# A two-layer decoder trunk on one core: the head reordered around modulation chunks, mixers and fillers

## The chip, the cores and the metric

The kernel runs on one core of a Trainium2 chip. The metric is the device time of one execution in microseconds. Three runs of the kernel before gave 560.85, 561.9 and 562.68 us; their median is 561.9 us.

## The reference

The input `x` is 256 tokens of 1024 channels, and `c` is one vector of 1024. Layer 0 mixes tokens by causal pooling, layer 1 by attention over one block of 256 tokens, and each is followed by a dense MLP with a squared ReLU.

```
c_act = silu(c)
for i in (0, 1):
    sh1, sc1, g1, sh2, sc2, g2 = split(c_act @ w_mod[i] + b_mod[i])     # six chunks of 1024
    h = rmsnorm(x, norm_mix[i]) * (1 + sc1) + sh1
    y = pool_mixer(h) if i == 0 else attention(h)
    x = x + g1 * y
    h = rmsnorm(x, norm_mlp[i]) * (1 + sc2) + sh2
    x = x + g2 * (relu(h @ w_up[i])**2 @ w_down[i])
out = rmsnorm(x, norm_final)

pool_mixer: channels in 4 groups of 256, windows 2, 4, 8, 16:
    (trailing mean of h over the window - h) @ w_pool[group], times pool_scale
```

## The kernel before

Activations stand transposed: 8 tiles of 128 channels by 256 tokens. All large weights come in transfers of 1 MB (16 tiles of 128x128) through SP's queue into five buffers (`RAW_BUFS`), in the order of `load_order` (L108). `issue` (L181) sends the next transfer; it is called when one has been used up, so transfer k+5 goes out once transfer k has been multiplied. A small transfer (a pool weight, or half of the first MLP weight) is sent along with the one ahead of it.

From the first MLP on, weights run as a stream: ScalarE casts each half transfer to a high part (`split_hi`, L250), VectorE subtracts to get a low part (`split_lo`, L256), and TensorE takes three matmuls for each tile (`mm_sum`, L274): high weights by high activations, high by low, low by high. `next_tile` (L620) hands out the tiles in a fixed order and runs whatever was put down for that tile by `later` (L612). This stream starts with the `m0u` matmuls (the first up-projection) and lasts to the end of the kernel.

The head is everything ahead of that stream, and the change lies in it. Its order on each engine is the order of the program; there is no planner. It does this:

- `cb` (L233 to L238): TensorE spreads silu(c) over all partitions, ScalarE copies it to `cact` (L553), for later chunks of the modulation that VectorE computes.
- The first norm: ScalarE squares `x` (L451), VectorE folds the squares by four adds (L452 to L455), TensorE sums them over partitions (`Rms.sums`, L376), ScalarE and VectorE take the reciprocal root (`rstd`, L386), TensorE spreads it (`spread`, L400), ScalarE copies it to `R` (`to_sbuf`, L408).
- The modulation of layer 0, as pairs of chunks. `PAIRS` (L50) names them: `sh0` to `sh3` are scale and shift of one channel group, `g32` and `g10` the gates of two groups each, `mlp0` to `mlp2` scale and shift for the MLP. A pair is two transfers, each holding half of the contraction for both chunks. `take` (L526) runs the products of one transfer (`pair_mm`, L302: 16 matmuls, 32 records) and calls `issue`. `given` (L529) lets VectorE pick the column out of the PSUM tile (`pair_out`, L313: four products, each with a read of its accumulator).
- For each channel group, 3 to 0: `normed` (L539) multiplies `x` by the root, `mixer` (L472) applies gain and shift on ScalarE and adds 4, 3, 2 or 1 shifted copies on VectorE, `pool_products` (L501) multiplies by the pool weights on TensorE. The loop at L543 finishes a group's mixer before it starts the next.
- `pool_out` (L514) adds the gated result to `x` and squares it, `pool_sums` (L522) sums the squares for the second norm `n1`; then `mlp0_in` (L593) makes the first MLP inputs, high and low part.
- `keep_warm` (L332) runs matmuls whose result nobody reads ("fillers"), at places chosen by hand.

Of the kernel before, what the change touches and what calls it, by code (L numbers as in the profile page):

```python
# [15 lines left out]
P = 128  # L16
# [91 lines left out]
def load_order():  # L108
    order = []

    def pair(name):
        order.extend(("c", name, i) for i in range(2))

    for j in GROUPS:
        pair(f"sh{j}")
        order.append(("p", j))
    pair("g32")
    pair("g10")
    order.append(("w0a",))
    pair("mlp0")  # L120
    order.extend([("w0b",), ("w", 1)])
    pair("mlp1")
    order.extend([("w", 2), ("w", 3)])
    pair("mlp2")
    order.extend([("w", 4), ("m", 0, 4, 3), ("m", 0, 3, 3), ("w", 5)])
    late = 0
    for h in range(HEAD_STEPS - AHEAD, N_STEPS):
        while late < len(LATE_STEPS) and LATE_STEPS[late] <= h:
            order.append(("m",) + LATE_MODS[late])
            late += 1  # L130
        if (h + AHEAD) % 2 == 0 and h + AHEAD < N_STEPS:
            order.append(("w", (h + AHEAD) // 2))
    return order
# [6 lines left out]
def tile_hybrid_pool_moba(  # L140
# [89 lines left out]
    nc.scalar.activation(ccol, vec[:, V_C : V_C + KD], AF.Silu)  # L230
    nc.scalar.activation(warm, ones, AF.Sqrt)
    cact = const.tile([P, D], F32, name="cact")
    cb = [bank(f"cb{i}") for i in range(2)]  # L233
    for k in range(KD):
        i, a = divmod(k, KD // 2)
        nc.tensor.matmul(
            cb[i][:, a * P : (a + 1) * P], ccol[:, k : k + 1].to_broadcast([P, P]), ident, start=True, stop=True
        )  # L238
# [60 lines left out]

    def pair_mm(name, half, region):  # L302
        w = loaded["c", name, half].rearrange("p (k q n) -> p k q n", k=KD // 2, q=4)
        for k in range(KD // 2):
            c0 = half * KD // 2 + k
            for q in range(4):
                nc.tensor.matmul(
                    region[32 * q : 32 * q + 32, :], ccol[:, c0 : c0 + 1].to_broadcast([P, 32]), w[:, k, q],
                    start=c0 == 0, stop=c0 == KD - 1, skip_group_check=True,
                )  # L310
        issue()

    def pair_out(name, region):  # L313
        for i, key in enumerate(PAIRS[name]):
            layer, m, j = key
            for a in range(2):
                t = tmp.tile([P, 32], F32, tag="pk", bufs=4, name="pk")
                nc.vector.scalar_tensor_tensor(
                    t, region[:, (2 * i + a) * 32 : (2 * i + a + 1) * 32], mod_bias(*key)[:, a : a + 1], pick,
                    op0=ALU.add, op1=ALU.mult, accum_out=mods[layer, m][:, 2 * j + a : 2 * j + a + 1],  # L320
                )
            known.add(key)
# [133 lines left out]
    pma = bank("pma")  # L456
    region = {f"sh{j}": pma[:, j * P : (j + 1) * P] for j in range(4)}
# [56 lines left out]
    def pool_out(g):  # L514
        cols = slice(2 * g, 2 * g + 2)
        nc.vector.tensor_mul(g1[:, cols], mods[0, 2][:, cols], vec[:, V_PSC + 2 * g : V_PSC + 2 * g + 2])
        for n in range(2):
            residual_sum(pools[g][:, n * S : (n + 1) * S], 2 * g + n, g1)
        sq1[g] = al_tile([P, 2, S], f"n1_sq{g}")
        nc.scalar.activation(sq1[g], x[:, 2 * g : 2 * g + 2], AF.Square)  # L520

    def pool_sums(g):  # L522
        for a in range(2):
            n1.sums(sq1[g][:, a], (g, a) == (0, 1))
# [4 lines left out]
    def given(name):  # L529
        pair_out(name, region[name])  # L530
# [3 lines left out]
    rms.spread()
    R = rms.to_sbuf()
    Rb = R.rearrange("p (a b) -> p a b", a=1).to_broadcast([P, 2, S])
    xr = [None] * 4

    def normed(g):  # L539
        xr[g] = al_tile([P, 2, S], f"n0_xr{g}")  # L540
        nc.vector.tensor_mul(xr[g], x[:, 2 * g : 2 * g + 2], Rb)

    for g, nxt in ((3, 2), (2, 1), (1, 0)):  # L543
        normed(g)
        given(f"sh{g}")
        if g == 3:
            keep_warm(2)
        take(f"sh{nxt}", 0)
        weave(mixer(g))
        if g == 3:  # L550
            keep_warm(2)
            for i in range(2):
                nc.scalar.copy(cact[:, i * D // 2 : (i + 1) * D // 2], cb[i])  # L553
        take(f"sh{nxt}", 1)
        pool_products(g)
    normed(0)
    given("sh0")
    weave(mixer(0))
    pool_products(0)
# [30 lines left out]
    gs01 = const.tile([P, KD], F32, name="gs0_4")  # L590


    def mlp0_in(j, R):  # L593
        gain(0, 4, V_NMLP, gs01, 2 * j, 2 * j + 2)
        sh = modv(0, 3, 2 * j)
        u = {}
        for k in (2 * j, 2 * j + 1):
            hl[k] = hl_tile(f"h01_{k}")
            u[k] = tmp.tile([P, S], F32, tag="h", bufs=2, name=f"h01_u{k}")
            nc.vector.scalar_tensor_tensor(u[k], xs[k], gs01[:, k : k + 1], R, op0=ALU.mult, op1=ALU.mult)  # L600
            nc.scalar.activation(hl[k][:, :S], u[k], AF.Identity, bias=sh[:, k : k + 1])
        for k in u:
            nc.vector.scalar_tensor_tensor(
                hl[k][:, S : 2 * S], u[k], sh[:, k : k + 1], hl[k][:, :S].bitcast(F32),
                op0=ALU.add, op1=ALU.subtract,
            )

    now = [0]
    due = {}
# [26 lines left out]
    def up(layer, hl, R):  # L636
        name = f"m{layer}u"
        g = (G_UP0, G_UP1)[layer]
        al = [None] * KF
        banks = {}  # L640

        def done(n):
            nm = f"{name}{n}"
# [46 lines left out]
        for n, k in UP_ORDER[layer]:  # L690
            w = next_tile()
            paired = R is None and n < g and n % 2 == 1
            if k == 0:
                banks[n] = banks[n - 1] if paired else bank(f"{name}{n}")
            t = hl[k]
            if R is None:
                a = S if paired else 0

                last = n % 2 == 1 or n >= g
                mm_sum(  # L700
                    banks[n][:, a : a + S], w, t[:, :S], t[:, S : 2 * S], k == 0 and a == 0, k == KD - 1 and last
                )
# [75 lines left out]
        return run  # L778

    def inputs(j):  # L780
        return lambda: mlp0_in(j, R1)

    mlp0_in(0, R1)
    R1 = n1.to_sbuf()
    split(1)
    head(2, splits(2))
    head(6, splits(3))
    head(12, take_late("mlp1", 0))
    head(19, take_late("mlp1", 1), lambda: given("mlp1"), inputs(1), splits(4))
# [312 lines left out]
```

## Time and profile before

| | |
|---|---|
| median of 3 runs | 561.9 us (560.85 to 562.68) |
| the profiled execution | 559.75 us, its span 558.0 us |
| granted clock, mean of the span | 0.983 |
| TensorE busy | 534.0 us, 96% |
| VectorE busy | 408.9 us, 73% |
| ScalarE busy | 323.1 us, 58% |
| read from HBM | 138.64 MB, 250 GB/s over the span |
| first `m0u` matmul | 60.94 us after the span's start |

The span runs from the first to the last instruction; the time of the execution includes what lies around it. Busy time of TensorE counts every matmul as long as its row says, at whichever clock it ran. The granted clock is 1.00 at full speed (2.4 GHz) and 0.50 at half (1.2 GHz); a value between is a mean over a stretch that holds both. An fp32 matmul has two records.

### The profile page before, as it was taken

To read this page: it belongs to the slowest core of one execution; us is meant where nothing else is said; L and a number is where in the kernel's file an instruction comes from. 1 tells how busy PE (TensorE), PEld (TensorE's weight loads), DVE (VectorE), ACT (ScalarE), POOL (GpSimd) and SP (SyncE) were. 2 spreads that over 40 slices of the span, in tenths; PEclk is the share of its full clock that TensorE was granted. 3 is DMA by queue.
4 is the path that set the end of the run, shared out by engine and by line. 5 is a ranking of instruction groups with operands and counts; after the bars stand their busy time and mean duration, and the time that the engine had idled before them with its cause. 6 is when DMAs were issued, how large, how long until landed. Compare 5 with 4: busy or idle time off the path is not lost.

```text
span 558.0 us, 10792 instructions
## 1 busy us (share of the span) xinstructions
PE 534.0 (96%) x4328; PEld 496.2 (89%) x4328; DVE 408.9 (73%) x830; ACT 323.1 (58%) x602; POOL 2.5 (0%) x18
## 2 busy tenths in 40 slices
PE   5777999999999999999999999999999999999995
PEld 4556899999998888899899999999999998888895
DVE  2644469689987998965899995686887786665641
ACT  3212234678754454454887878566897775444531
POOL 1000000000000000000000000000000000000000
PEclk9896899999999999999999999999999999999999
DMA  8998789748889989984377675434565477677002
GB/s 331 418 369 332 282 320 365 263 158 307 325 308 408 404 309 325 346 332 162 144 260 284 238 284 218 152 137 167 188 230 188 162 275 241 205 278 269 4 0 76
DMA packets 22338, 140.41 MB, mean 252 GB/s; under 512 B 2416, under 2 KB 4608, under 8 KB 5904
## 3 DMA queue, kind: packets, MB, share of 16 engines
q1 hardware_dynamic: 22048, 138.61, 67.5%
q10 hardware_dynamic: 144, 1.05, 0.5%
q8 instruction: 34, 0.56, 0.4%
q14 instruction: 16, 0.13, 0.1%
q0 software_dynamic: 96, 0.06, 0.0%
HBM read 138.64 MB, written 1.07 MB: 250 GB/s over the span
## 4 chain that ended last, share of the span: by engine, by line
PE 92%; DVE 4%; ACT 1%; DMA 1%; issue 1%; DVEq 0%
PE m1d L270 9%; PE m0d L270 9%; PE m1u L276 6%; PE m1u L277 6%; PE m1u L278 6%; PE m0u L276 6%; PE m0u L278 5%; PE m0u L277 5%; PE m0d L271 5%; PE m1d L271 5%; PE qkv L276 5%; PE qkv L277 4%; PE qkv L278 4%; PE wo L276 1%; PE n_rms L381 1%; PE wo L278 1%
## 5 line engine op out<-in xcount | busy, mean ns | idle before, releaser
L258 DVE TENSOR_TENSOR w_lo<-raw_w,w_hi 128x1024 fp32r<-128x1024 f32 x160 | 194.5, 1223 | 61.4 <-ACT w_hi L253 59.2
L253 ACT CAST w_hi<-raw_w 128x1024 fp32r<-128x1024 f32 x160 | 166.3, 1046 | 75.8 <-PE m1d L270 24.9
L270 PE MATMUL m1d<-m1u_al,w_hi 128*128 128x512 f32 x224 | 78.3, 393 | 0.0
L270 PE MATMUL m0d<-m0u_al,w_hi 128*128 128x512 f32 x224 | 78.2, 393 | 0.0
L292 DVE SCALAR_TENSOR_TENSOR raw_m<-raw_m,cact 128x1024 f32<-128x1024 f32 x60 | 72.9, 1217 | 0.0
L276 PE MATMUL m1u<-h_raw,w_hi 128*128 128x258 f32 x256 | 72.8, 284 | 0.0
L277 PE MATMUL m1u<-h_raw,w_hi 128*128 128x256 f32 x256 | 72.6, 284 | 0.0
L278 PE MATMUL m0u<-h,w_lo 128*128 128x256 f32 x256 | 71.8, 281 | 0.8 <-DVE w_lo L258 0.8
L278 PE MATMUL m1u<-h_raw,w_lo 128*128 128x258 f32 x256 | 72.5, 283 | 0.0
L276 PE MATMUL m0u<-h,w_hi 128*128 128x256 f32 x256 | 72.4, 283 | 0.0
L277 PE MATMUL m0u<-h,w_hi 128*128 128x256 f32 x256 | 71.7, 280 | 0.1
L271 PE MATMUL m0d<-m0u_al,w_lo 128*128 128x256 f32 x224 | 62.9, 281 | 0.0
L271 PE MATMUL m1d<-m1u_al,w_lo 128*128 128x256 f32 x224 | 62.8, 280 | 0.0
L276 PE MATMUL qkv<-h_raw,w_hi 128*128 128x258 f32 x192 | 57.4, 299 | 0.0
L277 PE MATMUL qkv<-h_raw,w_hi 128*128 128x256 f32 x192 | 54.6, 285 | 0.0
L278 PE MATMUL qkv<-h_raw,w_lo 128*128 128x258 f32 x192 | 54.4, 283 | 0.0
L270 PEld LDWEIGHTS m1d<-m1u_al,w_hi 128*128 128x128 f32 x224 | 42.1, 188 | 9.6
L270 PEld LDWEIGHTS m0d<-m0u_al,w_hi 128*128 128x128 f32 x224 | 42.1, 188 | 9.5
L276 PEld LDWEIGHTS m0u<-h,w_hi 128*128 128x128 f32 x256 | 48.2, 188 | 1.5 <-issue 1.2
L278 PEld LDWEIGHTS m0u<-h,w_lo 128*128 128x128 f32 x256 | 48.2, 188 | 1.0 <-DVE w_lo L258 1.0
L278 PEld LDWEIGHTS m1u<-h_raw,w_lo 128*128 128x128 f32 x256 | 48.8, 191 | 0.0
L276 PEld LDWEIGHTS m1u<-h_raw,w_hi 128*128 128x128 f32 x256 | 48.7, 190 | 0.0
(174 smaller groups left out, 984.1 us busy)
## 6 DMA issues: line engine op xcount, KB each, us to landing
raw_w<-in_w_all SPq DMA_DIRECT2D x79, 1024.0 KB, 6.1
raw_m<-in_w_mod SPq DMA_DIRECT2D x30, 1024.0 KB, 6.7
raw_c_sh<-in_w_mod SPq DMA_DIRECT2D x8, 1024.0 KB, 12.5
raw_c_mlp<-in_w_mod SPq DMA_DIRECT2D x6, 1024.0 KB, 5.7
raw_c_g<-in_w_mod SPq DMA_DIRECT2D x4, 1024.0 KB, 10.4
T<-bd SPq DMA_DIRECT2D x8, 256.0 KB, 8.9
x<-in_xT ACTq DMA_DIRECT2D x1, 1024.0 KB, 6.0
wp<-in_w_pool SPq DMA_DIRECT2D x4, 256.0 KB, 12.4
```

Source lines behind the costliest of these rows:

```text
L253: nc.scalar.copy(hi, raw)
L258: nc.vector.tensor_sub(lo, raw, hi.bitcast(F32))
L270: nc.tensor.matmul(b, hi, hl[:, : 2 * S], start=start, stop=False)
L271: nc.tensor.matmul(b[:, S:], lo, hl[:, :S], start=False, stop=stop)
L276: nc.tensor.matmul(dst, hi, xh, start=start, stop=False)
L277: nc.tensor.matmul(dst[:, :S], hi, xl, start=False, stop=False)
L278: nc.tensor.matmul(dst, lo, xh, start=False, stop=stop)
L292: nc.vector.scalar_tensor_tensor(raw[:, a], raw[:, a], 1.0, cact, op0=ALU.mult, op1=ALU.mult, accum_out=dst[:, a : a + 1])
L381: nc.tensor.matmul(self.bank[:, t : t + 1], sq[:, t * P : (t + 1) * P], ones, start=first and t == 0, stop=stop, skip_group_check=True,)
```

## The change

It touches only the head and the first eight tiles of the stream.

- `cb` moves from the start to behind the spread of the first norm, and its two copies to `cact` behind the first activations.
- The fillers read a tile of ones (`fill`) instead of the input vectors. Seven run first of all on TensorE; the later ones stand at other places and in other numbers (two groups of three between takes, and so on).
- The first norm has two adds on VectorE instead of four, and TensorE sums four tiles instead of one. VectorE multiplies by the root out of PSUM, without `to_sbuf`.
- All four `normed` stand together. The mixers run overlapped: a group's gain and activations are issued before the group ahead of it has finished its adds, and each pair's takes stand on TensorE ahead of the products of an earlier group.
- `g10` and `mlp0` are packed by chunk (`BY_VECTOR`): one transfer holds the whole contraction of one chunk, so a chunk can be picked after its own take. `pair_out` handles one chunk at a time.
- After the gates, residuals and sums are ordered by chunk; squares are per 128 channels instead of per 256.
- `mlp0` is loaded ahead of both halves of the first weight transfer.
- The first input of the MLP is split into steps, with the cast of the first weights between them; the first eight tiles of the stream run in three passes (`mm_sums`): all high by high, then all high by low, then all low by high.

```diff
+BY_VECTOR = {"g10", "mlp0"}
...
     pair("g10")
-    order.append(("w0a",))
     pair("mlp0")
-    order.extend([("w0b",), ("w", 1)])
+    order.extend([("w0a",), ("w0b",), ("w", 1)])
...
-    cb = [bank(f"cb{i}") for i in range(2)]
-    for k in range(KD):
...
+    def mm_sums(todo):
+        for i in range(3):
+            for dst, w, xh, xl, start, stop in todo:
+                nc.tensor.matmul(
+                    dst, w[i // 2], xl if i == 1 else xh, start=start and i == 0, stop=stop and i == 2
+                )
...
+    fill = act.tile([P, 2, S], F32, tag="T", bufs=NP, name="fill")[:, 0]
+    nc.vector.memset(fill, 1.0)
...
-            nc.tensor.matmul(junk[0][:, :S], ident, vec[:, :S], start=True, stop=True)
+            nc.tensor.matmul(junk[0][:, :S], fill[:, :P], fill, start=True, stop=True)
...
+    keep_warm(7)
     for i in range(4):
         nc.scalar.activation(sq[i], x[:, 2 * i : 2 * i + 2], AF.Square)
...
-    nc.vector.tensor_add(sq[0], sq[0], sq[2])
-    nc.vector.tensor_add(sq[0][:, 0], sq[0][:, 0], sq[0][:, 1])
...
-    keep_warm(4)
+    for a in range(2):
+        rms.sums(sq[0][:, a], False)
     pair_mm("sh3", 0, region["sh3"])
-    rms.sums(sq[0][:, 0], True)
+    for a in range(2):
+        rms.sums(sq[2][:, a], a == 1)
...
     rms.rstd()
     take("sh3", 1)
-    rms.spread()
-    R = rms.to_sbuf()
-    Rb = R.rearrange("p (a b) -> p a b", a=1).to_broadcast([P, 2, S])
+    both_given("sh3")
+    R = rms.spread().rearrange("p (a b) -> p a b", a=1).to_broadcast([P, 2, S])
+
+    cb = [bank(f"cb{i}") for i in range(2)]
+    for k in range(KD):
...
-    for g, nxt in ((3, 2), (2, 1), (1, 0)):
...
+    normed(3)
+    m = [mixer(g) for g in range(4)]
+    next(m[3])
+    for g in (2, 1, 0):
         normed(g)
...
+    take("sh2", 0)
+    keep_warm(3)
+    take("sh2", 1)
+    keep_warm(3)
+    next(m[3])
+    next(m[3])
+    both_given("sh2")
+    next(m[2])
+    weave(m[3])
+    take("sh1", 0)
+    pool_products(3)
+    take("sh1", 1)
+    keep_warm(1)
+    weave(m[2])
+    both_given("sh1")
+    next(m[1])
+    pool_products(2)
+    take("sh0", 0)
+    keep_warm(3)
+    take("sh0", 1)
+    weave(m[1])
+    both_given("sh0")
+    next(m[0])
+    pool_products(1)
...
     take("g32", 0)
     keep_warm(2)
+    weave(m[0])
     take("g32", 1)
-    given("g32")
+    pool_products(0)
+    both_given("g32")
     pool_out(3)
     pool_out(2)
-    keep_warm(1)
     take("g10", 0)
+    given("g10", 0)
+    pool_out(1)
     pool_sums(3)
     pool_sums(2)
     take("g10", 1)
-    w0 = split_hi(0)
-    given("g10")
-    pool_out(1)
+    given("g10", 1)
     pool_out(0)
     pool_sums(1)
+    keep_warm(1)
     pool_sums(0)
-    split_lo(0, *w0)
     n1.rstd()
     take("mlp0", 0)
+    given("mlp0", 0)
+    gs01 = const.tile([P, KD], F32, name="gs0_4")
+    gain(0, 4, V_NMLP, gs01, 0, 2)
+    R1 = n1.spread()
     take("mlp0", 1)
-    given("mlp0")
-    R1 = n1.spread()
     junk[0] = bank("junk2")
     keep_warm(2)
...
+    first = Input(0)
+    first.scaled(R1)
+    given("mlp0", 1)
+    w0 = split_hi(0)
+    first.high()
+    first.low(0)
+    split_lo(0, *w0)
+    first.low(1)
     R1 = n1.to_sbuf()
     split(1)
```

## Rows read from the trace of the kernel before

**Rows 1.** Busy by stage: PE, PEld, DVE, ACT, POOL; granted clock, DMA share, GB/s.

```profile
20.00:38.00 18.00, 12.28 (x170) 9.33 (x163) 13.25 (x50) 3.27 (x6) 0.00 (x0) 0.91 1.01 418
38.00:61.00 23.00, 19.58 (x246) 16.25 (x244) 8.98 (x46) 4.34 (x8) 0.00 (x0) 0.70 0.75 284
61.00:549.00 488.00, 487.12 (x3741) 457.95 (x3740) 377.76 (x704) 305.25 (x569) 0.49 (x1) 1.00 0.67 242
```

**Rows 2.** TensorE's waits, 61 to 558 us: us in total, times, longest.

```profile
PE m0u L278 <- DVE w_lo L258: 0.8, 1, 0.8
```

**Rows 3.** Timeline of TensorE, 5 to 38 us: start, duration, instruction, count.

```profile
6.29 3.63 PE L236 MATMUL cb<-vec,ccol 128*128 128x128 f32 x16 [6.29 <-ACT ccol L230]
...
9.76 1.89 PE L334 MATMUL junk<-vec 128*128 128x256 f32 x8
...
14.41 0.71 PE L402 MATMUL n_rms<-vec,n_r 128*128 128x128 f32 x4 [0.20 <-DVE n_r L398]
...
19.35 1.08 PE L307 MATMUL pma<-raw_c_sh,ccol 128*32 128x128 f32 x32 [0.22 <-DMA raw_c_sh<-in_w_mod]
...
28.25 1.99 PE L506 MATMUL pool<-pd,wp 128*128 128x256 f32 x8 [0.32 <-DVE pd L497]
```

**Rows 4.** Weight loads of cb and n_rms: ns min/median/max, first and last start.

```profile
L236 PEld LDWEIGHTS cb<-vec,ccol x16: 285/333/333, 6.3 to 9.4; 128*128 128x128 f32 x16
L402 PEld LDWEIGHTS n_rms<-vec,n_r x4: 185/188/189, 14.4 to 14.7; 128*128 128x128 f32 x4
```

**Rows 5.** Timeline of all engines, 0 to 45 us.

```profile
8.83 0.69 DVE L452 TENSOR_TENSOR n_sq<-n_sq,n_sq 128x512 f32<-128x512 f32 x1 [7.93 <-ACT n_sq L451]
...
13.24 0.26 ACT L389 ACTIVATE n_s<-n_rms,epsc 128x2 f32<-128x2 f32 x1 [3.41 <-PE n_rms L381]
...
14.20 0.16 DVE L398 SCALAR_TENSOR_TENSOR n_r<-n_q,n_y 128x2 f32<-128x2 f32 x1
...
22.89 0.24 DVE L318 SCALAR_TENSOR_TENSOR pk<-pma,vec 128x32 f32<-128x32 f32 x1
...
23.77 1.09 ACT L479 ACTIVATE ph<-n_xr,mod,gs 128x256 f32<-128x256 f32 x2 [4.68 <-DVE gs L349]
...
25.69 1.49 DVE L486 TENSOR_TENSOR win<-win 128x512 f32<-128x512 f32 x2
...
28.02 0.17 DVE L497 TENSOR_TENSOR pd<-pe,ph 128x14 f32<-128x14 f32 x1
...
43.52 0.88 DVE L445 SCALAR_TENSOR_TENSOR x<-pool,g1p,x 128x256 f32<-128x256 f32 x2
...
44.42 0.63 ACT L520 ACTIVATE n_sq<-x 128x512 f32<-128x512 f32 x1 [8.73 <-DVE x L445]
```

**Rows 6.** Timeline of TensorE, 44 to 61 us.

```profile
45.11 2.03 PE L381 MATMUL n_rms<-ones,n_sq 128*128 128x1 f32 x16 [0.56 <-ACT n_sq L520]
...
51.53 3.57 PE L381 MATMUL n_rms<-ones,n_sq 128*128 128x1 f32 x16 [2.58 <-ACT n_sq L520]
...
55.03 3.64 PE L307 MATMUL pmb<-raw_c_mlp,ccol 128*32 128x128 f32 x64
...
58.60 1.22 PE L402 MATMUL n_rms<-vec,n_r 128*128 128x128 f32 x4
...
60.94 0.43 PE L276 MATMUL m0u<-h,w_hi 128*128 128x256 f32 x1
```

**Rows 7.** Busy time and granted clock around the two falls.

```profile
20.30:22.40 2.10, 0.13 (x7) 0.00 (x0) 1.93 (x6) 0.00 (x0) 0.00 (x0) 1.00 1.02 423
...
23.30:26.70 3.40, 3.40 (x34) 2.37 (x36) 2.03 (x10) 1.09 (x2) 0.00 (x0) 0.50 1.02 426
...
47.20:60.80 13.60, 11.02 (x119) 9.76 (x116) 6.23 (x31) 1.95 (x5) 0.00 (x0) 0.50 0.70 261
```

**Rows 8.** SP's timeline: the issue of the last gate transfer.

```profile
31.32 0.33 SPq L204 DMA_DIRECT2D raw_c_g<-in_w_mod  x1
```

**Rows 9.** DMA issues, 29.5 to 32 us: count, KB each, median us to landing.

```profile
raw_c_g<-in_w_mod SPq DMA_DIRECT2D x1, 1024.0 KB, 10.0
```

More of the change, by code (lines that the diff above doesn't have):

```diff
@@ L298, in mod_dve, with pair_mm @@
             issue()
[L302 to L305, printed above, removed]
+    def pair_mm(name, i, region):
+        whole = name in BY_VECTOR
+        nk = KD if whole else KD // 2
+        w = loaded["c", name, i].rearrange("p (k q n) -> p k q n", k=nk, q=4)
+        cols = slice(64 * i, 64 * i + 64) if whole else slice(0, P)
+        for k in range(nk):
+            c0 = k if whole else i * nk + k
             for q in range(4):
                 nc.tensor.matmul(
-                    region[32 * q : 32 * q + 32, :], ccol[:, c0 : c0 + 1].to_broadcast([P, 32]), w[:, k, q],
+                    region[32 * q : 32 * q + 32, cols], ccol[:, c0 : c0 + 1].to_broadcast([P, 32]), w[:, k, q],
                     start=c0 == 0, stop=c0 == KD - 1, skip_group_check=True,
@@ L311, in pair_mm, with pair_out @@
         issue()
[L313 to L322, printed above, removed]
+    def pair_out(name, i, region):
+        key = PAIRS[name][i]
+        layer, m, j = key
+        for a in range(2):
+            t = tmp.tile([P, 32], F32, tag="pk", bufs=4, name="pk")
+            nc.vector.scalar_tensor_tensor(
+                t, region[:, (2 * i + a) * 32 : (2 * i + a + 1) * 32], mod_bias(*key)[:, a : a + 1], pick,
+                op0=ALU.add, op1=ALU.mult, accum_out=mods[layer, m][:, 2 * j + a : 2 * j + a + 1],
+            )
+        known.add(key)
     def mod(*key):
@@ L518, in pool_out, with given, both_given @@
             residual_sum(pools[g][:, n * S : (n + 1) * S], 2 * g + n, g1)
[L519 to L520 removed]
+            sq1[2 * g + n] = al_tile([P, S], f"n1_sq{2 * g + n}")
+            nc.scalar.activation(sq1[2 * g + n], xs[2 * g + n], AF.Square)
     def pool_sums(g):
[L523 to L524 removed]
+        for n in range(2):
+            n1.sums(sq1[2 * g + n], (g, n) == (0, 1))
     def take(name, half):
         pair_mm(name, half, region[name])
[L529 to L530 removed]
+    def given(name, i):
+        pair_out(name, i, region[name])
+    def both_given(name):
+        for i in range(2):
+            given(name, i)
     rms.rstd()
     take("sh3", 1)
[L534 to L536 removed]
+    both_given("sh3")
+    R = rms.spread().rearrange("p (a b) -> p a b", a=1).to_broadcast([P, 2, S])
+    cb = [bank(f"cb{i}") for i in range(2)]
+    for k in range(KD):
+        i, a = divmod(k, KD // 2)
+        nc.tensor.matmul(
+            cb[i][:, a * P : (a + 1) * P], ccol[:, k : k + 1].to_broadcast([P, P]), ident, start=True, stop=True
+        )
     xr = [None] * 4
@@ L540, in normed @@
         xr[g] = al_tile([P, 2, S], f"n0_xr{g}")
-        nc.vector.tensor_mul(xr[g], x[:, 2 * g : 2 * g + 2], Rb)
-    for g, nxt in ((3, 2), (2, 1), (1, 0)):
-        normed(g)
[L545 to L559, printed above, removed]
+        nc.vector.tensor_mul(xr[g], x[:, 2 * g : 2 * g + 2], R)
+    normed(3)
+    m = [mixer(g) for g in range(4)]
+    next(m[3])
+    for g in (2, 1, 0):
+        normed(g)
+    for i in range(2):
+        nc.scalar.copy(cact[:, i * D // 2 : (i + 1) * D // 2], cb[i])
+    take("sh2", 0)
[22 more added lines that the diff above has]
+    pool_products(1)
     pmb = bank("pmb")
@@ L589, in tile_hybrid_pool_moba, with __init__, gain, scaled @@
     hl = [None] * KD
[L590 to L602, printed above, removed]
+    class Input:
+        def __init__(self, j):
+            self.ks = (2 * j, 2 * j + 1)
+            self.u = {}
+        def gain(self):
+            gain(0, 4, V_NMLP, gs01, self.ks[0], self.ks[1] + 1)
+        def scaled(self, R):
+            for k in self.ks:
+                self.u[k] = tmp.tile([P, S], F32, tag="h", bufs=2, name=f"h01_u{k}")
+                nc.vector.scalar_tensor_tensor(self.u[k], xs[k], gs01[:, k : k + 1], R, op0=ALU.mult, op1=ALU.mult)
+        def high(self):
+            sh = modv(0, 3, self.ks[0])
+            for k in self.ks:
+                hl[k] = hl_tile(f"h01_{k}")
+                nc.scalar.activation(hl[k][:, :S], self.u[k], AF.Identity, bias=sh[:, k : k + 1])
+        def low(self, k):
             nc.vector.scalar_tensor_tensor(
-                hl[k][:, S : 2 * S], u[k], sh[:, k : k + 1], hl[k][:, :S].bitcast(F32),
+                hl[k][:, S : 2 * S], self.u[k], modv(0, 3, k)[:, k : k + 1], hl[k][:, :S].bitcast(F32),
                 op0=ALU.add, op1=ALU.subtract,
             )
+        def all(self, R):
+            self.gain()
+            self.scaled(R)
+            self.high()
+            for k in self.ks:
+                self.low(k)
     now = [0]
@@ L640, in up @@
         banks = {}
+        first_tiles = []
         def done(n):
@@ L699, in up @@
                 last = n % 2 == 1 or n >= g
-                mm_sum(
-                    banks[n][:, a : a + S], w, t[:, :S], t[:, S : 2 * S], k == 0 and a == 0, k == KD - 1 and last
-                )
+                args = (banks[n][:, a : a + S], w, t[:, :S], t[:, S : 2 * S], k == 0 and a == 0, k == KD - 1 and last)
+                if k == 0 and n < HALF:
+                    first_tiles.append(args)
+                    if n == HALF - 1:
+                        mm_sums(first_tiles)
+                else:
+                    mm_sum(*args)
             else:
@@ L788, in tile_hybrid_pool_moba @@
     head(12, take_late("mlp1", 0))
-    head(19, take_late("mlp1", 1), lambda: given("mlp1"), inputs(1), splits(4))
+    head(19, take_late("mlp1", 1), lambda: both_given("mlp1"), inputs(1), splits(4))
     head(23, splits(5))
```

21 lines of the change are left out of this document (10 added, 11 removed).

## The prediction

> **What bounds the kernel now.** I read the stages first [rows 1]. From 61 us to 549 us TensorE is busy 487.12 of 488.00 us at the full granted clock, and its waits there come to 0.8 us [rows 2]. That stretch is bound by TensorE's own instructions, and the change leaves their number alone; a start of the stream that is x us earlier ends the kernel x us earlier, as long as its weights arrive. Ahead of it stands the head, 60.94 us long, to the last row of [rows 6], where TensorE is busy 19.58 of 23.00 us in its last part and yet late, because the granted clock has a mean of 0.70 there. So the question is when the first `m0u` matmul starts.
>
> In the head three things set the pace. Transfers: in 20 to 38 us the DMA engines are full at 418 GB/s [rows 1], 2.5 us for each 1 MB; the last gate transfer lands at 31.32 + 10.0 = 41.3 us [rows 8, 9]. VectorE: each group's mixer follows the one before, with TensorE idle in between (0.13 busy of 2.10 us at 20.3) [rows 7]. The clock: it falls to half (0.50) at 23.3, after that idle stretch, and is 0.50 from 47.2 to 60.8 [rows 7], having fallen as TensorE came out of the sums of squares, 16 records with one column each [rows 6].
>
> The clock column is not enough for the start. It says 1.00 from the first us, but the weight loads of `cb` at 6.3 us have a median of 333 ns, against 188 ns for the same 128x128 load at 14.4 us [rows 4]. So the core starts at the half level, and the 16 records of `cb` and the fillers behind them [rows 3] are what brought it to full before the first norm. The Trainium skill says the same of the start (TensorE: Matmul & The Clock Gate, Part 1, What's actually happening: the throttled state is the default, and activity releases it), and warns under Seeing it yourself that single clock events of a trace are not to be trusted fully. The trace agrees with both.
>
> **Prices.** At full clock, and at half where a row shows it: the 32 records of one transfer ("a take") 1.0 us (the row at 19.35) [rows 3] and 1.8 us (64 records 3.64) [rows 6]; sums of two groups 2.0 and 3.6 [rows 6]; a spread 0.7 [rows 3] and 1.2 [rows 6]; a filler matmul 0.43 (8 records, 1.89 with the tail) [rows 3]; products of a group 2.0 [rows 3]. VectorE: picking a pair and its gain 0.9 (22.89 to 23.77), a window add 0.75, a mixer behind its activations 3.3 for three adds (24.87 to 28.19), so 2.6 for two and 1.8 for one; the activations 1.1; root and Newton chain 1.1 (13.24 to 14.36); two residuals 0.9; a square of 128x512 0.63, so 0.4 for half of it [rows 5].
>
> **Part A, to the end of the take of sh2's second half (call it T).** The early fillers start at about 1.2 us instead of 9.76 and are over by 7 us at either clock (14 records, some of them at twice 0.215 us). Then TensorE has nothing until the first add of squares is done at 8.83 + 0.69 = 9.5 us. `cb` no longer stands there: it moves behind the spread, onto TensorE's path. At full clock: sums 1.0, take 1.0, sums 1.0 (12.5), chain 1.1 with the next take beside it (13.6), spread 0.7 (14.4), `cb` 2.0 by the sums' 16 loads of the same size (16.4), take 1.0 and three fillers 1.3 (18.7); sh2's second half lands at 19.35 [rows 3], so T = 20.3. At half from the sums on: 9.5 + 3 x 1.8 = 14.9, take 16.7, spread 17.9, `cb` 3.6 [rows 3] 21.5, then 1.0 + 1.3 + 1.0 at full: T = 24.8. The idle stretch from 7 to 9.5 us is longer than the 2.1 us ahead of the fall at 23.3, and only sums and one take follow it, so I take the half clock, back to full somewhere in `cb`: T = 23.5, with 20.3 and 24.8 kept as ends.
>
> [...]
>
> Edits of part A at no price of their own: three of VectorE's adds become more sums; the copy of R to SBUF goes (0.4 us), but VectorE multiplies from PSUM; both lie ahead of T, which TensorE sets. VectorE's four multiplications by R (0.7 each) now stand together behind the spread and end beside `cb`. If that cover went, up to 2 us of them would show.
>
> **Part B, the pipelined mixers, to the end of the take of g32's second half.** In VectorE's queue from T: picking and gain 0.9, the rest of group 3's mixer 2.6 (its first two adds are done), group 2's 3.3 with its activations beside: T + 6.8. From there TensorE's queue is longer: products of group 2 2.0, take 1.0, three fillers 1.3, take 1.0, products of group 1 2.0, take 1.0, two fillers 0.9, take 1.0: T + 17.0. VectorE fits under it: 0.9 + 1.1 + 2.6 has group 1 ready at T + 11.4 against T + 12.1; 0.9 + 1.1 + 1.8 has group 0 at T + 15.9. Transfers are no wait here: g32's second half is two transfers ahead of the last gate transfer and lands two steps of 2.5 us ahead of 41.3, at 36.3, and its take starts at T + 16.0 = 39.5. What is new is that VectorE's queue holds picks that wait for TensorE's takes, and behind them the next mixer: a slow TensorE stops both.
>
> **Part C, to the first m0u matmul, at full clock.** Products of group 0 2.0, take 1.0, sums 2.0, take 1.0 (6.0); half a pick 0.35, gate 0.15, residuals 0.9 (7.4); square 0.4, last sums 0.5 (8.3); chain 1.1 beside mlp0's first take (9.4); spread 0.7, take 1.0, half a pick 0.4, activation 0.5: 12.0. The split picks and squares are in it. Now the clock. Before, it fell as TensorE ran two groups' sums with one take ahead; here four groups' sums stand within one stretch with one take and one filler among them, so I expect the fall again. Half clock for sums, filler, sums (+2.0), a take (+0.8), spread (+0.5) and the other take (+0.8) costs up to 4.0; I take 2.5, since the fall can come anywhere in the stretch.
>
> **Sum.** 23.5 + 17.0 + 12.0 + 2.5 = 55.0, and 0.7 for some ten hand-overs of under 0.1 us (14.36 to 14.41 is one): 55.7, against 60.94. That is 5.2 us; a stream that starts before the clock is fully back gives 0.5 of it up, and the passes give 0.3 back (between nothing and 0.43, the length of the first matmul, whose successor waited; the low weights are now wanted 16 matmuls later). I take 5.0. The profiled execution took 559.75 us (span 558.0, with 1.75 around it): 554.75. The median shown is 561.9, 2.15 above it; with the same difference, 556.9.
>
> **Queues.** SP sends transfer k+5 when take k has been done. w0 now follows mlp0: at 2.5 us each after 41.3, mlp0 lands at 43.8 and 46.3, w0's halves at 47.6 and 48.8, w1 at 51.3, mlp1 at 53.8 and 56.3. The takes that release them come 8 to 10 us ahead of these times, so the queue does not run dry. With the first matmul at 55.7 all are hidden. At 50 they would still be: its cast needs 47.6 + 1.0. The picks of mlp1 are due 19 tiles into the stream, 7 us later.
>
> **Rivals.**
> The clock holds in one of the two places, or in both. For it: fillers are added. Against: both places hold sums and idleness. With T = 20.3 and no late fall, 20.3 + 29.0 + 0.7 = 50.0, 10.9 us: 551.0. With one fall 7 to 8 us: about 554.3. Chance 0.28.
> The change gains nothing (0.12): the low clock lasts into the products of group 2 and one take (3.0 us of work, +2.4) on top of both ends, 24.8 + 29.0 + 4.0 + 0.7 = 58.5, so 60.9: 561.9.
> Slower (0.10), the same mechanism further: takes alone need not bring the clock back. From 55.0 to 58.6 us TensorE ran nothing else and stayed at 0.50 [rows 6, 7]. If it stays low to the end of part B, TensorE's 10.2 us there become 18.4: 66.7 us, 5.8 later, 567.7. It decides from the point where the clock is not back by about 37 us.
> Late transfers: if w0 came 5 us behind its forecast it would cost a start at 50 some 4 us and one at 55.7 nothing; it lies inside the range.
>
> **How the numbers follow.** My case (falls in both places, 2.5 to 6.5 us gained) has 0.50. Faster by over 0.3% (1.7 us, about what can be told from no change) is 0.50 + 0.28 = 0.78, same 0.12, slower 0.10. The range goes from 551.0, both clocks kept, to 561.0, the case of no gain, and leaves out the slower case and a little at each end.
>
> **What would show it.** T between 20.3 and 24.8 us, weight loads of `cb` near 333 ns at about 18 us; sums at 3.6 us per two groups and a spread of 1.2 us just ahead of the stream; first m0u matmul near 55.7; from there the same length to the end as before, 497 us. It is wrong if `cb` runs at 188 ns, if the stream starts early and then waits for weights, or if TensorE waits for VectorE in part B.

## The result and the profile after

The changed kernel takes 554.0 us (median of 4 runs, 553.39 to 555.03); the kernel before, with one more run, 561.4 us. The ratio is 0.9867, 95% interval 0.9841 to 0.9893: 7.4 us less by the medians. The two profiled executions differ by less, 559.75 and 555.03 us: of its kernel's runs listed here the one of before is the fastest, the one of after the slowest. The prediction was worked out in the first of them, so its terms are held against the second; the medians come back at the end.

By stage, as in [rows 1] (columns: PE, PEld, DVE, ACT, POOL, granted clock, DMA share, GB/s):

```profile
20.00:38.00 18.00, 17.09 (x239) 12.96 (x238) 11.03 (x45) 3.60 (x7) 0.00 (x0) 1.00 1.01 417
38.00:56.00 18.00, 18.00 (x375) 15.60 (x374) 9.82 (x48) 4.98 (x12) 0.00 (x0) 0.81 0.91 337
56.00:544.00 488.00, 487.13 (x3739) 457.90 (x3738) 378.60 (x705) 305.39 (x570) 0.49 (x1) 1.00 0.66 243
```

The stream from 56 us on is what it was from 61 us on: 487.13 of 488.00 us busy, full clock. The first m0u matmul starts at 56.15 us instead of 60.94, and from there it is 497.0 us to the end (553.2 - 56.15), before 497.1 (558.0 - 60.94). So the whole difference of the two spans, 4.8 us, lies in the head. One pair of executions shows this; how far the executions of one kernel differ is told below.

TensorE's timeline of the head, against [rows 3, 6]:

```profile
1.25 5.86 PE L342 MATMUL junk<-fill 128*128 128x256 f32 x14 [1.25 <-DVE fill L337]
...
9.21 1.27 PE L389 MATMUL n_rms<-ones,n_sq 128*128 128x1 f32 x8 [2.11 <-DVE n_sq L463]
...
15.94 1.22 PE L410 MATMUL n_rms<-vec,n_r 128*128 128x128 f32 x4
...
16.95 3.47 PE L553 MATMUL cb<-vec,ccol 128*128 128x128 f32 x16
...
22.86 1.08 PE L313 MATMUL pma<-raw_c_sh,ccol 128*32 128x128 f32 x32
...
27.35 1.99 PE L515 MATMUL pool<-pd,wp 128*128 128x256 f32 x8 [0.91 <-DVE pd L506]
...
30.82 1.89 PE L515 MATMUL pool<-pd,wp 128*128 128x256 f32 x8
...
40.15 1.08 PE L313 MATMUL pmb<-raw_c_g,ccol 128*32 128x128 f32 x32
...
44.11 1.95 PE L389 MATMUL n_rms<-ones,n_sq 128*128 128x1 f32 x16
...
47.02 1.51 PE L389 MATMUL n_rms<-ones,n_sq 128*128 128x1 f32 x8
...
49.38 1.71 PE L389 MATMUL n_rms<-ones,n_sq 128*128 128x1 f32 x8
...
51.02 1.93 PE L313 MATMUL pmb<-raw_c_mlp,ccol 128*32 128x64 f32 x64
...
52.88 1.22 PE L410 MATMUL n_rms<-vec,n_r 128*128 128x128 f32 x4
...
54.03 1.18 PE L313 MATMUL pmb<-raw_c_mlp,ccol 128*32 128x64 f32 x64
...
56.15 2.18 PE L279 MATMUL m0u<-h,w_hi 128*128 128x256 f32 x16
```

The early fillers end at 7.1 us; the first sums start at 9.21; `cb` stands behind the spread; the take at 22.86 is sh2's second half, so T, the end of that take, is 23.9 us; g32's second take ends at 41.2; the sums from 47.02 on, 8 records each, take 1.51 and 1.71 us where 16 take 1.95 at full clock (44.11); the spread takes 1.22 us.

The weight loads of `cb` (ns min/median/max, first and last start), against [rows 4]:

```profile
L553 PEld LDWEIGHTS cb<-vec,ccol x16: 283/333/333, 16.7 to 19.9; 128*128 128x128 f32 x16
```

And the clock around the two stretches in which it was at half, against [rows 7]:

```profile
7.10:9.20 2.10, 0.00 (x1) 0.00 (x0) 0.69 (x1) 2.09 (x6) 0.00 (x0) 1.00 0.96 394
9.90:20.10 10.20, 10.20 (x95) 9.21 (x95) 4.68 (x20) 1.82 (x4) 0.00 (x0) 0.50 1.01 405
44.10:47.40 3.30, 3.30 (x92) 3.18 (x84) 1.71 (x10) 1.13 (x4) 0.00 (x0) 1.00 1.03 348
47.50:54.20 6.70, 6.70 (x92) 6.11 (x95) 2.48 (x16) 2.00 (x4) 0.00 (x0) 0.50 0.80 304
```

TensorE did nothing from 7.1 to 9.2 us, and from 9.9 to 20.1 us the clock is 0.50: `cb`, moved into that stretch, ran at 333 ns for each load. At the end TensorE is busy without a gap from 44.1 to 47.4 us, mostly with one-column sums and a take, and falls to 0.50 nevertheless until 54.2 us.

### The profile page after: what moved, and what is told of

The parts are those of the page before. It is cut to its first block, busy times and chain, and to the rows that moved or that the text cites. A ratio compares the mean times of both kernels' runs of the same rounds, so it can differ in the third digit from the quotient of the medians.

```text
span 553.2 us, 11110 instructions
## 1 busy us (share of the span) xinstructions
PE 541.8 (98%) x4486; PEld 503.3 (91%) x4486; DVE 408.1 (74%) x829; ACT 323.4 (58%) x605; POOL 2.5 (0%) x18
## 3 DMA queue, kind: packets, MB, share of 16 engines
q10 hardware_dynamic: 144, 1.05, 0.5%
## 4 chain that ended last, share of the span: by engine, by line
PE 90%; DVE 4%; ACT 3%; issue 1%; DMA 1%; DVEq 0%; ACTq 0%
PE m0d L264 9%; PE m1d L264 9%; PE m1u L271 5%; PE m1u L272 5%; PE m1u L273 5%; PE m0d L265 5%; PE m1d L265 5%; PE qkv L271 5%; PE m0u L271 5%; PE m0u L273 5%; PE m0u L272 4%; PE qkv L272 4%; PE qkv L273 4%; PE pma L313 2%; PE n_rms L389 2%; PE pool L515 1%
## 5 line engine op out<-in xcount | busy, mean ns | idle before, releaser
L247 ACT CAST w_hi<-raw_w 128x1024 fp32r<-128x1024 f32 x160 | 166.2, 1046 | 74.9 <-PE m1d L264 24.8
L273 PE MATMUL m0u<-h,w_lo 128*128 128x256 f32 x248 | 69.6, 281 | 0.8 <-DVE w_lo L252 0.8
L271 PE MATMUL m0u<-h,w_hi 128*128 128x256 f32 x248 | 70.0, 282 | 0.0
L272 PE MATMUL m0u<-h,w_hi 128*128 128x256 f32 x248 | 69.4, 280 | 0.0
L271 PEld LDWEIGHTS m1u<-h_raw,w_hi 128*128 128x128 f32 x256 | 48.7, 190 | 0.0
L272 PEld LDWEIGHTS m1u<-h_raw,w_hi 128*128 128x128 f32 x256 | 48.5, 190 | 0.0
L271 PEld LDWEIGHTS m0u<-h,w_hi 128*128 128x128 f32 x248 | 46.7, 188 | 1.3 <-issue 1.2
```

What stands on the lines that cost most here:

```text
L247: nc.scalar.copy(hi, raw)
```

## The experiments

A ratio is to the kernel before, run beside it on the same chip, with a median between 559.2 and 562.44 us. The last column is the profiled execution alone.

| run | what it is | median us | ratio (95%) | first m0u, us |
|---|---|---|---|---|
| after | the changed kernel | 554.0 | 0.9867 (0.9841 to 0.9893) | 56.15 |
| e1 | twelve early fillers | 553.45 | 0.9869 (0.984 to 0.9897) | 54.92 |
| e2 | cb in front | 551.16 | 0.9826 (0.98 to 0.9851) | 51.79 |
| e3 | mixers in series | 559.72 | 0.9974 (0.9954 to 0.9994) | 60.36 |
| e4 | last part as before | 556.09 | 0.9915 (0.9888 to 0.9941) | 57.98 |
| e5 | no passes | 553.67 | 0.9851 (0.9825 to 0.9878) | 57.97 |
| e6 | w0 ahead of mlp0 | 553.98 | 0.9853 (0.9827 to 0.9878) | 54.92 |
| e7 | e2, g10's takes adjacent | 551.83 | 0.9811 (0.979 to 0.9832) | 53.08 |
| e8 | e2, 8 fillers fewer | 550.96 | 0.9806 (0.9785 to 0.9827) | 53.38 |
| e9 | e7, squares folded by GpSimd | 552.67 | 0.9874 (0.9847 to 0.9901) | 54.87 |
| e10 | no early fillers | 554.98 | 0.9912 (0.988 to 0.9944) | 55.72 |
| e11 | e9, pick between the takes | 551.33 | 0.9805 (0.9789 to 0.9821) | 51.23 |
| e12 | e7, pick between the takes | 551.52 | 0.9812 (0.9795 to 0.983) | 54.84 |

Each kernel's own runs spread over 1 to 6 us, more than several of the differences. Medians that differ by under 2 us with overlapping runs tell nothing apart; the trace then shows where the time went, in one execution. The ratios have a noise of their own: the runs of the kernel before gather near 559 and near 562.4 us, beside e9 and e10 mostly near 559, beside e5 to e8, e11 and e12 mostly near 562.4. That alone moves a ratio by 0.006, so ratios are best compared among rows that were run together.

**e1, more early fillers.**

```diff
-    keep_warm(7)
+    keep_warm(12)
```

> Twelve early fillers instead of seven, so that TensorE is busy from 1.3 to about 9.2 us instead of 7. Theory (the clock falls at 9.9 us because TensorE stood idle from 7.1 to 9.2 us): cb's weight loads come down from 333 ns towards 188 ns, the take of sh2's second half ends near 20.5 to 21.5 us instead of 23.9, the first m0u starts 2.5 to 3.5 us earlier than 56.15 us, the time is about 551 us. Rival 1 (the sums of squares pull the clock down whatever stands ahead of them): cb at 333 ns again, take at 23.5 to 24, 554 us. Rival 2 (transfers set the pace behind the mixers): cb fast, take early, but first m0u gains under 0.7 us, 553.5 to 554 us.

```profile
9.14 1.05 PE L389 MATMUL n_rms<-ones,n_sq 128*128 128x1 f32 x8 [1.00 <-DVE n_sq L463]
...
11.17 1.87 PE L389 MATMUL n_rms<-ones,n_sq 128*128 128x1 f32 x8
...
21.19 1.08 PE L313 MATMUL pma<-raw_c_sh,ccol 128*32 128x128 f32 x32
...
50.89 1.60 PE L313 MATMUL pmb<-raw_c_mlp,ccol 128*32 128x64 f32 x62
...
53.73 0.30 PE L313 MATMUL pmb<-raw_c_mlp,ccol 128*32 128x64 f32 x2 [1.24 <-issue]
...
54.92 2.17 PE L279 MATMUL m0u<-h,w_hi 128*128 128x256 f32 x16
```

The twelve fillers did not close the idle stretch: 1.00 us is left of 2.11 (9.14). The first sums and the first take ran at full clock (1.05 and 1.12 us), and then the clock fell all the same: the second sums, 8 records, took 1.87 us at 11.17, and the loads of `cb` have a median of 333 ns again. The take ends at 22.2 us, 1.7 earlier, neither theory's number. The fall comes at 11 instead of 9.9, but in e3, with 3.49 us of idleness there, it came at 11.3; idleness and sums are not told apart by this run. A gain of 0.55 us in the median is within the spread. In this trace a second thing ate part of it: the last take stands still for 1.24 us two records before its end (53.73, put down to issue, so no engine or transfer that the profile shows). I did not find its cause, and no other trace that I read has it.

**e2, cb in front.**

```diff
     keep_warm(7)
+    cb = [bank(f"cb{i}") for i in range(2)]
+    for k in range(KD):
...
     R = rms.spread().rearrange("p (a b) -> p a b", a=1).to_broadcast([P, 2, S])
-    cb = [bank(f"cb{i}") for i in range(2)]
-    for k in range(KD):
```

> cb goes back ahead of the first sums, behind the seven fillers; all else as in the changed kernel. Theory (cb on TensorE's path and the half clock cost 3.4 us up to the take of sh2's second half): cb runs from about 7 to 9 us, where TensorE was idle, the take ends at 20.4 to 21 us (its transfer lands near 19.4), first m0u 3 to 3.5 us earlier, 550.5 to 551 us. Rival (that time is lost again to transfers of the last gates or to a clock that falls later): 553.5 to 554 us.

```profile
6.49 1.95 PE L462 MATMUL cb<-vec,ccol 128*128 128x128 f32 x16
...
15.48 1.67 PE L313 MATMUL pma<-raw_c_sh,ccol 128*32 128x128 f32 x32 [1.92 <-DMA raw_c_sh<-in_w_mod]
...
17.08 2.60 PE L342 MATMUL junk<-fill 128*128 128x256 f32 x6
...
19.61 1.08 PE L313 MATMUL pma<-raw_c_sh,ccol 128*32 128x128 f32 x32
...
51.79 2.34 PE L279 MATMUL m0u<-h,w_hi 128*128 128x256 f32 x16
```

The theory's numbers hold. `cb` fills the hole from 6.5 to 8.4 us and takes 1.95 us instead of 3.47; all sums and takes up to 12.6 us run at full clock; T is 20.6 us, and the first take of sh2 now waits 1.92 us for its transfer. 2.8 us of median (551.16 against 554.0, with no run of the one as slow as the fastest of the other; 2.3 by the ratios) is what the move of `cb` cost the change.

The clock is not kept, though. Behind that wait it is 0.50 from 15.9 to 19.2 us, and three fillers take 2.60 us instead of 1.56. The five later kernels with this start show what counts. e7:

```profile
11.71 1.94 PE L313 MATMUL pma<-raw_c_sh,ccol 128*32 128x128 f32 x32
...
18.93 1.08 PE L313 MATMUL pma<-raw_c_sh,ccol 128*32 128x128 f32 x32 [0.80 <-DMA raw_c_sh<-in_w_mod]
```

In e7, e8 and e11 the clock fell at 11 to 12.2 us and stayed at half for 3 to 10 us; in e9 and e12 it stayed at 1.00. T is 19.9, 20.0 and 20.3 us in the first three, 20.2 and 20.5 in the other two, and in all five sh2's second take waits 0.6 to 1.4 us for its transfer. So T became earlier because `cb` left TensorE's path, up to where the transfer lands; a kept clock is not needed for it.

**e3, mixers in series.**

```diff
-    normed(3)
     m = [mixer(g) for g in range(4)]
-    next(m[3])
-    for g in (2, 1, 0):
+    for g, nxt in ((3, 2), (2, 1), (1, 0)):
         normed(g)
...
+        if g < 3:
+            both_given(f"sh{g}")
+        if g == 3:
+            keep_warm(2)
+        take(f"sh{nxt}", 0)
+        weave(m[g])
+        if g == 3:
+            keep_warm(2)
...
+        take(f"sh{nxt}", 1)
+        pool_products(g)
```

> The four mixers one after the other, with the takes between them, as in the kernel before; start and last part as in the changed kernel. Theory (the pipelining brings about 1 us, the last part most of the gain): products of group 0 end near 41.5 us, g32's second take near 44.5 us instead of 41.2, first m0u 1 to 3 us later than 56.15, 555 to 557 us. Rival (pipelining is the whole gain): 560 to 561.4 us, no faster than before.

```profile
22.09 1.08 PE L313 MATMUL pma<-raw_c_sh,ccol 128*32 128x128 f32 x32
...
37.98 3.15 PE L515 MATMUL pool<-pd,wp 128*128 128x256 f32 x8 [2.25 <-issue]
...
43.57 1.08 PE L313 MATMUL pmb<-raw_c_g,ccol 128*32 128x128 f32 x32
...
60.36 2.17 PE L279 MATMUL m0u<-h,w_hi 128*128 128x256 f32 x16
```

My theory after the first comparison was that pipelining brings 1 us. It came from reading the two traces at one point: g32's second take ends at 42.5 us before (T + 22.1, with T = 20.4 there) and at 41.2 after. That is refuted: in series the time is 559.72 us, 5.7 us more, close to the rival's 560, and the interval of the ratio nearly reaches 1. From the end of sh2's second take to the end of g32's second it is 21.5 us here (23.1 to 44.6), 17.3 us pipelined. The start, 3.5 us later than before, had hidden this. TensorE idles 2.2 us ahead of the last products, which then take 3.15 us instead of 1.99: in series, the clock falls in the mixers too. So the price of the series is not waiting alone: of the 4.2 us between 21.5 and 17.3, some 1.6 are products and a take at half clock (3.15 and 1.52 us instead of 1.99 and 1.08). The run also has six fillers fewer between the takes. In the pipelined order fewer fillers cost nothing in the median (e8); in series that was not run.

**e4, the last part as before.**

```diff
-BY_VECTOR = {"g10", "mlp0"}
+BY_VECTOR = {"mlp0"}
...
+    keep_warm(1)
     take("g10", 0)
-    given("g10", 0)
-    pool_out(1)
     pool_sums(3)
     pool_sums(2)
     take("g10", 1)
-    given("g10", 1)
+    both_given("g10")
+    pool_out(1)
     pool_out(0)
     pool_sums(1)
-    keep_warm(1)
     pool_sums(0)
```

> The last part as before: g10 packed by halves of the contraction, both its takes ahead of picking, group 1's residuals behind them, no filler between the last sums. Theory (3.5 of the 4.8 us between the two profiles come from this part): first m0u at 58.5 to 59.5 us, 556.5 to 558 us. Rival (the gain was made ahead of g32's second take): within 0.7 us of the changed kernel, 553.5 to 554.7 us.

```profile
46.21 1.08 PE L313 MATMUL pmb<-raw_c_g,ccol 128*32 128x128 f32 x32
...
49.28 3.14 PE L389 MATMUL n_rms<-ones,n_sq 128*128 128x1 f32 x16 [2.00 <-ACT n_sq L529]
...
57.98 2.17 PE L279 MATMUL m0u<-h,w_hi 128*128 128x256 f32 x16
```

2.1 us in the median, 1.8 us at the first m0u, a little under the theory's numbers: with both chunks of g10 picked behind the second take, TensorE waits 2.00 us for the squares of group 1 (49.28), and then runs both groups' sums in one piece. By the medians the last part is worth about 2 us, the mixers in the new order about 5.7.

**e5, no passes; e6, w0 ahead of mlp0.** In e5 the eight tiles call `mm_sum` one by one; in e6 `load_order` has `("w0a",)` ahead of `pair("mlp0")` again.

> The first eight tiles tile by tile, three matmuls each, instead of in three passes; all else as in the changed kernel. In its trace the first low weights are done 1.6 us after the first m0u matmul (56.53 + 1.22 against 56.15), and the third matmul would then wait for them. Theory (the passes hide that): a wait of about 1.1 us on the low weights at the third matmul, tiles 8 on about 1 us later, 554.7 to 555.5 us against 554.0. Rival (the prediction: 0.3 us, and the following split catches up): within 0.4 us of the changed kernel.

> The first half of the first MLP weights is sent ahead of mlp0 again, as before; all else as in the changed kernel. Theory (these transfers are hidden in either order, mlp0 landing 7 us ahead of its take): first m0u within 0.5 us of 56.15, time 553.5 to 554.6 us. Rival (mlp0 was a transfer on the path): first m0u 1 us later, 555 us.

The third matmul of e5, then the last sums and the first `m0u` of e6:

```profile
59.19 0.39 PE L273 MATMUL m0u<-h,w_lo 128*128 128x256 f32 x1 [0.63 <-DVE w_lo L252]
```

```profile
46.85 1.05 PE L390 MATMUL n_rms<-ones,n_sq 128*128 128x1 f32 x8
...
49.68 1.70 PE L314 MATMUL pmb<-raw_c_mlp,ccol 128*32 128x64 f32 x64
...
54.92 2.18 PE L280 MATMUL m0u<-h,w_hi 128*128 128x256 f32 x16
```

In e5 the third matmul waits 0.63 us for the low weights, as the theory says, though less. Its median shows nothing of it (553.67); this profiled execution is that kernel's slowest run. What 0.6 us are worth the time cannot tell. e6 has the changed kernel's time, 553.98 us, as predicted, but its first m0u starts 1.23 us earlier, which neither theory nor rival has. Its last sums still run at full clock (1.05 us where the changed kernel has 1.51 and 1.71); the clock falls only in the take behind them. The earlier start lies mostly in that, and the column of first m0u holds such differences between executions.

**e7, g10's takes adjacent; e8, fewer fillers**, both on top of e2.

```diff
     take("g10", 0)
+    take("g10", 1)
     given("g10", 0)
     pool_out(1)
     pool_sums(3)
     pool_sums(2)
-    take("g10", 1)
     given("g10", 1)
```

> On top of the kernel with cb in front (551.16 us): both takes of g10 stand together, ahead of the sums of groups 3 and 2, which held the second one back by 1.9 us. Its transfer lands near 41 us. Theory (the second take of g10, its pick, residuals, squares and last sums are the chain into the stream): the take ends at 42.0 to 42.3 instead of 43.8, first m0u 1.0 to 1.8 us earlier than 51.79, 549.3 to 550.3 us. Rival (TensorE's own queue of sums and takes is the chain, so their order is indifferent): first m0u within 0.5 us of 51.79, 550.7 to 551.5 us.

> On top of the kernel with cb in front (551.16 us): without the three fillers between sh2's takes, the three between sh0's and the two between g32's, 8 of 0.43 us each on TensorE's path. Theory (fillers of part B cost their own length, and the clock holds without them since takes and products stand densely): g32's second take ends 2 us earlier than 37.9, then g10's second transfer, landing near 41 us, keeps all but about 1 us of it: 550 to 550.5 us. Rival (the clock falls inside the mixers without them): half clock somewhere in 20 to 38 us, 553 to 556 us.

VectorE in e2, then TensorE and VectorE in e7:

```profile
41.02 0.25 DVE L324 SCALAR_TENSOR_TENSOR pk<-pmb,vec 128x32 f32<-128x32 f32 x1 [0.21 <-PE pmb L313]
```

```profile
41.23 1.10 PE L313 MATMUL pmb<-raw_c_g,ccol 128*32 128x64 f32 x64 [0.67 <-DMA raw_c_g<-in_w_mod]
...
42.40 0.25 DVE L324 SCALAR_TENSOR_TENSOR pk<-pmb,vec 128x32 f32<-128x32 f32 x1 [2.26 <-PE pmb L313]
```

The second take comes 1.5 us earlier than in e2 and nothing follows from it: the first pick, at 41.02 us in e2, now starts at 42.40, when the second take is done. Both takes write one PSUM tile, and the order of the program had put the pick behind both. The theory failed, for a reason that I had not seen, and the rival's numbers did not come either: the first m0u is 1.3 us later than in e2 (53.08), the median 551.83 us, with half clock from about 45.8 us. e8 removes 8 fillers (3.4 us of TensorE) and its median stays with e2's. g32's second take ends at 36.2 us instead of 37.9, near the theory's 2 us, though it waits 1.0 us for its transfer; then the clock falls already at about 41.7 us, and the first m0u is 1.6 us later than in e2 (53.38).

**e9, e11, e12: fewer sums, and the pick in its place.** In e9, on top of e7, GpSimd adds the two squares of groups 3, 2 and 1 (`nc.gpsimd.tensor_add`), and TensorE sums 5 tiles instead of 8. e11 and e12 change the order of e9 and e7 to this:

```diff
     take("g10", 0)
-    take("g10", 1)
     given("g10", 0)
+    take("g10", 1)
     pool_out(1)
-    pool_sums(3)
-    pool_sums(2)
     given("g10", 1)
     pool_out(0)
+    pool_sums(3)
+    pool_sums(2)
```

> On top of the kernel with cb in front and g10's takes adjacent (551.83 us, ratio 0.9811): GpSimd adds the two squares of groups 3, 2 and 1, so TensorE sums 5 tiles for the second norm instead of 8 (20 records fewer to 12 fewer: 20 instead of 32). Theory (TensorE's own queue of sums is the chain of the last part, and its one-column matmuls let the clock fall): sums end 1 to 1.5 us earlier at full clock, 2 to 3 us earlier where they ran at half, 549 to 550.5 us, ratio 0.976 to 0.979. Rival (VectorE's residuals and squares are the chain, or GpSimd's adds are slow and late): no earlier than 46.5 us for the end of the sums, ratio 0.981 or above.

> On top of the kernel with folded squares: the pick of g10's first chunk stands between its two takes, the group's residuals right behind, and the sums follow both picks. In the two kernels before it the first pick waited for the second take (both write one PSUM tile) and started at 42.2 to 42.4 us instead of 41.0. Theory (that wait, and GpSimd's add behind it, undid the earlier take): last squares near 44.3 us, sums done near 45 to 45.5 us, first m0u at 50.5 to 51.5 us, 549.5 to 550.5 us. Rival (one-column sums close together bring the clock down whatever the order, and TensorE's takes at half clock set the end): first m0u at 52.5 us or later, 551.5 to 552.7 us.

> The same order without GpSimd's adds (eight tiles summed by TensorE), on top of the kernel with adjacent takes. Theory: the pick starts at 41.0 us, the second take waits 0.4 us for it, but 4 us of sums stand behind: they end at 46.3 to 47 us, as with cb in front alone (46.6), 550.5 to 551.5 us, so that the fold is what is worth 1 us in the run beside it. Rival (the sums are hidden, the residuals were the chain): sums done by 45.5 us, 549.5 to 550.5 us.

TensorE in e9, then VectorE and GpSimd in e11:

```profile
45.08 1.01 PE L389 MATMUL n_rms<-ones,n_sq 128*128 128x1 f32 x4 [1.93 <-POOL n_sq L537]
```

```profile
40.70 0.25 DVE L324 SCALAR_TENSOR_TENSOR pk<-pmb,vec 128x32 f32<-128x32 f32 x1 [0.22 <-PE pmb L313]
...
41.01 0.72 POOL L537 TENSOR_TENSOR n_sq<-n_sq,n_sq 128x256 f32<-128x256 f32 x1 [0.24 <-ACT n_sq L535]
...
41.16 0.58 DVE L531 TENSOR_TENSOR g1p<-mod,vec 128x2 f32<-128x2 f32 x1
```

The pick is back at 40.7 us, and the sums end at 46.0 us in e11 and at 48.6 us in e12, later than either theory has them; e11's first m0u, at 51.23, is its theory's. The medians do not tell the two apart (551.33 and 551.52), nor from e2. e9 is no faster than e7: its TensorE waited 1.93 us for GpSimd's add of group 1, behind the late pick, as its rival has it. What separates e12's trace from e2's is for the most part the clock. Two stretches of the same 10.5 us, first in e2, then in e12:

```profile
44.70:55.20 10.50, 10.25 (x175) 8.92 (x175) 6.79 (x23) 6.08 (x10) 0.00 (x0) 0.84 1.02 418
```

```profile
44.70:55.20 10.50, 10.50 (x155) 9.51 (x156) 3.38 (x18) 2.52 (x7) 0.00 (x0) 0.52 0.95 371
```

In e2 the mean is 0.84, the half clock lasts from 46.5 to about 49.9 us; in e12 it lasts nearly through. e12's order is the better one by VectorE's rows, and its profiled execution, the slowest of its runs, starts the stream 3.05 us later. Whether the closer sums bring the fall forward is not shown by one trace of each. I have no version that reliably beats e2; e2, e7, e8, e11 and e12 lie together at 550.96 to 551.83 us, and e2 has the simplest edit and the narrowest spread (550.71 to 551.85).

**e10, no early fillers**: the line `keep_warm(7)` is left out.

> The changed kernel without the seven early fillers; nothing else. Theory (they end at 7 us, TensorE idles to 9.2, the clock is down again by the first take, so they buy next to nothing): cb at 333 ns as with them, the take of sh2's second half at 24 to 25 us, time within 0.7 us of the changed kernel, ratio 0.986 to 0.988. Rival (they carry the first sums and the first take at full clock and shorten the half-clock stretch): 1.5 to 3 us slower, ratio 0.990 to 0.992.

1.0 us in the median, with overlapping ranges (553.79 to 556.55 against 553.39 to 555.03), between theory and rival. The first m0u is no later (55.72 us). The ratio suggests more, 0.9912 against 0.9867, but the kernel before stood at 559.2 us beside it. So the early fillers alone buy little, about 1 us by the medians. What they do with `cb` behind them was not run.

## Why the prediction was right, step by step

**Part A** (T = 23.5, ends 20.3 and 24.8): 23.9 measured. The fall behind the early fillers, `cb` at half and the return inside `cb` came as written. The other end was reached as well, with `cb` in front: T is 20.6 us in e2. It did not need the kept clock that the prediction gave as its condition: in e2, e7, e8 and e11 the clock fell and T is 19.9 to 20.6 all the same, because `cb` was off the path. What I did not ask was whether the half clock comes from idleness or from the sums. It stays open: e1 left 1.00 us of idleness.

**Part B** (17.0): 17.3 measured. TensorE waits once for VectorE, 0.91 us ahead of group 3's products (27.35). The prediction had named such a wait as a sign of being wrong; but this one lies in the first 6.8 us, where its own sum has VectorE lead, and group 2's products start at 30.82, against T + 6.8 = 30.7. From there TensorE runs without a wait, as forecast. Here the prediction added up the new order but never said what the old one took over the same stretch, so it did not see that pipelining was the largest single gain. e3 supplied that.

**Part C** (12.0, 2.5 for the fall, 0.7 for hand-overs: 15.2): 14.9 measured. The fall came, at 47.4 us.

**The sum**: first m0u at 55.7 forecast, 56.15 measured; 5.0 us forecast, 4.8 measured between the two spans. The half microsecond for a slow start of the stream was not needed, the clock was back at 54.3. The passes were mis-sized: the wait that they hide is 0.63 us in e5, above the prediction's 0.3 and its bound of 0.43, though no median shows it. The order of w0 shows no cost in the time (e6). The rival of late transfers was put on w0 and did not come; once past the start, TensorE waited for transfers only in the kernels with `cb` in front: up to 1.92 us for sh2 and up to 1.03 us for a gate. That the sum meets this one trace to half a microsecond is in part luck: the runs of the changed kernel differ by 1.6 us, and the profiled one is the slowest. In the fastest the first m0u would stand near 54.5, an estimate from 56.15 less the 1.64 us between the two times.

**The median**: 556.9 forecast, 554.0 measured, inside the range. The mis-sized term is the step from the profiled execution to the median. I added the 2.15 us by which the one lay under the other before; after, the profiled run lies 1.0 us above its median. So 7.4 us are 4.7 between the two executions, 1.65 by which the one lay under its kernel's median, and 1.0 by which the other lay above. That is also more than the 2.5 to 6.5 us of the case that the prediction gave 0.50; the time lies where it had put one fall, about 554.3, while the trace shows both. The difference is no constant of the program. The mean clocks below point to where the falls of the clock lay in each execution as its cause; with one trace of the kernel this is argued, not shown.

## What to carry to other kernels

Work that TensorE has to do anyway is a good filler: put into a hole where the engine waits, it leaves the path, while the same work behind the hole ran at half clock and in the way (2.8 us here). Whether it also holds the clock differed between executions. Compare two orders over the same stretch, from one shared event to another, and not at one moment: a start 3.5 us later hid most of the gain from pipelining (5.7 us by e3's median). And when an earlier transfer or take brings nothing, look at what the next reader really waits for; here it was a second writer of the same PSUM tile.

## What the runs showed of the hardware

- A TensorE that is busy by its rows can still lose the clock. In the changed kernel it was busy 3.30 of 3.30 us ahead of the fall at 47.4, in sums of one column each (16 records at 44.11, the next from 47.02) and a take between them; in e1 the fall at 11 came behind sums and a take, with 1.00 us of idleness ahead of them. The Trainium skill (TensorE: Matmul & The Clock Gate, Part 1, What's actually happening) has the gate set by how busy the engine has been. The first fall, behind an idle stretch, agrees with that; the one at 47.4 does not, if busy is what these rows count as busy.
- At the start the fall went with idleness ahead of the first sums, in single executions. It came behind them, at 11 to 12.2 us, in e7, e11, e8 and e1, where TensorE had waited 0.67, 0.80, 0.92 and 1.00 us. It did not come there in e9, e2 and e12, where TensorE had waited nothing, 0.16 and 0.32 us. These are too few executions to call it the cause.
- The falls move between executions. The second fall came at 47.4 us in the changed kernel and at 50.0 us, in the take from 49.68 on, in e6, whose TensorE work in the head is the same. The four runs of the changed kernel have a mean clock of 0.984 at 553.39 and 553.5 us, and of 0.981 at 554.51 and 555.03.
- While GpSimd added two 128x256 tiles (0.7 us each), a VectorE product of two columns took 0.58 us instead of 0.16 (e11, 41.16 us), and ended when the add did. The Trainium skill (GPSIMD Engine Reference, 1. Specifications) says that the two engines share SBUF interfaces, and that VectorE's instructions with two SBUF inputs contend for them. The trace agrees, with 0.4 us for this one.
